# Moving the gates' running sums from VectorE to ScalarE and GpSimd, rebuilding the activation quarters from split halves, and four column chunks instead of five

## The chip, the cores and the metric

The kernel runs on one core of one Trainium2 chip. Its time is the device time of one execution in microseconds, from the first to the last instruction and what the device adds around it. Three runs of the kernel before took 1839.42, 1838.30 and 1839.01 us (median 1839.01 us).

The engines are called PE (TensorE, matrix products), DVE (VectorE), ACT (ScalarE), POOL (GpSimd) and SP (SyncE, which only issues transfers here). Each engine works through its own instructions in a fixed order, and a wait of one instruction holds all that stand behind it on that engine.

## The reference, cut to what matters

Two groups of tokens (128 context tokens and 512 latent tokens, 640 in all, width 1024) go through two layers with the same weights. Each layer:

```
mod = silu(cond) @ ada_w + ada_b                 # six vectors of 1024 per token group
sh_m, sc_m, g_m, sh_f, sc_f, g_f = six slices of mod
h = rmsnorm(x, norm_mix) * (1 + sc_m) + sh_m
y = token_mixers(h)                              # 4 gated-recurrence heads, 4 retention heads, w_out
x = x + g_m * y                                  # gate of the mixer
h = rmsnorm(x, norm_ffn) * (1 + sc_f) + sh_f
gate, up = split(h @ w_up)                       # 2 x 2816 columns
x = x + g_f * ((silu(gate) * up) @ w_down)       # gate of the feed-forward part
```

The vectors `g_m` and `g_f` are needed as rows of 1024 that lie on all 128 partitions, since `x` has tokens on the partitions. There are two of each per layer, one for each token group.

## The kernel before, in words

All products are done in pieces of full precision: an operand is split into a rounded part ("hi") and the rest ("lo"), and hi·hi, hi·lo and lo·hi are added up in PSUM. For the weights, `Stream.cut` does the split: the cast to `wh` on ACT (L103) and the subtraction to `wl` on DVE (L104). There are six raw weight buffers in the second layer and four split ones, and PE's use of a split buffer frees it.

A scheduler gives every engine its order ahead of time. What decides it here is the order in which the program emits the work (a main loop, with side lanes that advance one step each few microseconds of main work) and the scheduler's own estimate of when things are ready; buffer pools add waits.

**The gates** (`ada_gate`, `ada_chunk`) are a side lane. Each gate has two column halves of 512. For each half eight tiles `adw` (128 x 512 of `ada_w`, one for each k) are loaded through SP into the pool `adp`. DVE multiplies a tile by the condition's column k and adds it to `acc`, once for each token group: L510 for k = 0, L512 (one multiply-add) for the other seven. Then `hl`, the split of `acc` (L567, L568), goes through a product with a matrix of ones (`pg`, L571 and L572), which sums over the partitions and writes the sum on all of them; L574 adds it to the row `gate`. That is 128 DVE instructions for the two gates of both layers. The pool `adp` has two buffers; it also gives `sg` in `g_unit` and `xa` in `x_add`. The feed-forward gate (lane name `gf`) has to be finished in emission order before the first `w_down` pass of the layer, and the `pg` products of its second half stand in PE's order directly ahead of that pass.

**The feed-forward part.** In the first layer all 22 column blocks (128 columns of gate and of up each) are done plainly (`ws`). In the second layer only two are; the other 20 go through `seven`, which computes a pair of blocks from seven products instead of eight by sums of halves of the tokens and halves of the input width. `seven` needs four combinations `E` of four quarters `F` of the activations (a quarter is half of the tokens by half of the width, 128 x 1280 elements). `combos` (L654 to L657) forms them on DVE, `combo` splits each into hi (L665 on ACT) and lo (L666 on DVE). `combo_last` makes the one that PE's third product in a pair (`y0`, PSUM tile `sy`) reads, and writes it into a quarter of `hT`. PE's second product reads `E[2]`.

**The norm ahead of it.** After `w_out`, each of the five token tiles is normed, transposed on PE (`pt`, L598), scaled and shifted and split into `hT`. In the first layer `norm_c` does so through a temporary `full`. In the second `norm_f` writes the scaled values to the four quarters `hf` as well, so that they exist when `combos` starts; the tile t = 2 lies in both token halves and is done in two pieces of 64 columns.

**Chunks.** The 22 blocks are done in chunks (`CH`): after the blocks of a chunk, their rows of `w_down` are applied and the result is added to `x` (`x_add`, L1113 and L1115, 128 x 512 at a time; the last chunk does its second half in two times 256 columns). In the second layer there are five chunks of 5, 5, 4, 4 and 4 blocks, so the first holds the two plain blocks and three from `seven`.

Of the kernel before, what the change touches and what calls it, by code (L numbers as in the profile page):

```python
# [10 lines left out]
F32 = mybir.dt.float32  # L11
F32R = mybir.dt.float32r
I32 = mybir.dt.int32
AF = mybir.ActivationFunctionType
ALU = mybir.AluOpType
AX = mybir.AxisListType

P = 128
DM = 1024
KT = DM // P  # L20
NT = 5
TOK = NT * P
HALF = TOK // 2
# [4 lines left out]
NF = DFF // P  # L28
# [3 lines left out]
RAW_BUFS = 3  # L32
W_BUFS = 4
B_BUFS = 13
CH = ((11, 11), (5, 5, 4, 4, 4))
PLAIN = (NF, 2)
HK = KT // 2
LATE = "r2"
# [9 lines left out]
CUT = 256  # L48
Q_SCAN = 2.65
Q_ADA = (3.0, 2.0, 4.0)  # L50
ADP_BUFS = 2
BOOT_LOADS = (
    "L00 x4 L01 L10 L02 L11 L12 L13 L03 L20 x2 x3 x0 x1 L21 L30 L22 L31 L32 L33 L23 W W W "
).split()
# [93 lines left out]
class Net:  # L148
    def __init__(self, ctx, tc, a, o):
# [8 lines left out]
        self.wlp = pool("wlp", W_BUFS)  # L158
        self.adp = pool("adp", ADP_BUFS)
        self.smp = pool("smp", 4)  # L160
# [339 lines left out]
    def ada_chunk(self, l, col, alloc, sink):  # L500
        nc, a = self.nc, self.a
        acc = alloc("acc")
        for k in range(KT):
            w = self.adp.tile([P, 512], F32, tag="ad", name="adw")
            nc.sync.dma_start(out=w, in_=a["ada_w"][l, k * P:(k + 1) * P, col:col + 512])
            for c in range(2):
                d = acc[:, 512 * c:512 * c + 512]
                s = self.sT[:, c, k:k + 1]
                if k == 0:
                    self.pin(nc.vector.tensor_scalar(d, w, s, None, op0=ALU.mult))  # L510
                else:
                    nc.vector.scalar_tensor_tensor(d, w, s, d, op0=ALU.mult, op1=ALU.add)  # L512
            yield
        yield from sink(acc)

# [84 lines left out]

    def norm_c(self, t, src, l, m):
        nc = self.nc
        if m == 1 and PLAIN[l] < NF:
            return self.norm_f(t, src, l, m)
        km = KT // 2
        c = 0 if t == 0 else 1
        full = self.ON("full")
        fv = full[:, :DM].rearrange("p (k n) -> p k n", k=KT)
        sv = src[:, :DM].rearrange("p (k n) -> p k n", k=KT)
        G, S = self.modc[:, l, m, 0, c], self.modc[:, l, m, 1, c]  # L610
        hi, lo = self.hT[:, 0, :, t * P:(t + 1) * P], self.hT[:, 1, :, t * P:(t + 1) * P]
        for k in range(km):
            nc.scalar.activation(fv[:, k], sv[:, k], AF.Identity, bias=S[:, k:k + 1], scale=G[:, k:k + 1])
        bc = lambda v: v[:, km:].unsqueeze(2).to_broadcast([P, KT - km, P])
        nc.vector.tensor_tensor(fv[:, km:], sv[:, km:], bc(G), op=ALU.mult)
        nc.vector.tensor_tensor(fv[:, km:], fv[:, km:], bc(S), op=ALU.add)
        for a, b in ((0, km), (km, KT)):
            nc.scalar.copy(hi[:, a:b], fv[:, a:b])
            nc.vector.tensor_tensor(lo[:, a:b], fv[:, a:b], hi[:, a:b].bitcast(F32), op=ALU.subtract)

    def norm_f(self, t, src, l, m):
        nc = self.nc
        c = 0 if t == 0 else 1
        sv = src[:, :DM].rearrange("p (k n) -> p k n", k=KT)
        G, S = self.modc[:, l, m, 0, c], self.modc[:, l, m, 1, c]
        a = 0
        while a < P:
            h = (t * P + a) // HALF
            b = min(P, (h + 1) * HALF - t * P)
            n, o = b - a, t * P + a - h * HALF  # L630
            for kh in range(2):
                if (h, kh) not in self.F:
                    self.F[h, kh] = self.B("hf")
                fv = self.F[h, kh].rearrange("p (k n) -> p k n", k=HK)[:, :, o:o + n]
                ks = slice(HK * kh, HK * kh + HK)
                if kh == 0:
                    for k in range(HK):
                        nc.scalar.activation(fv[:, k], sv[:, k, a:b], AF.Identity, bias=S[:, k:k + 1],
                                             scale=G[:, k:k + 1])
                else:  # L640
                    bc = lambda v: v[:, ks].unsqueeze(2).to_broadcast([P, HK, n])
                    nc.vector.tensor_tensor(fv, sv[:, ks, a:b], bc(G), op=ALU.mult)
                    nc.vector.tensor_tensor(fv, fv, bc(S), op=ALU.add)
                hi, lo = (self.hT[:, d, ks, t * P + a:t * P + b] for d in range(2))
                nc.scalar.copy(hi, fv)
                nc.vector.tensor_tensor(lo, fv, hi.bitcast(F32), op=ALU.subtract)
            a = b

    def quarter(self, h, kh):
        return [self.hT[:, d, HK * kh:HK * kh + HK, h * HALF:(h + 1) * HALF] for d in range(2)]  # L650

    def combos(self):
        V, F = self.nc.vector, self.F
        V.tensor_tensor(F[1, 0], F[1, 1], F[1, 0], op=ALU.subtract)  # L654
        V.tensor_tensor(F[0, 0], F[0, 0], F[1, 0], op=ALU.add)
        V.tensor_tensor(F[1, 1], F[0, 0], F[1, 1], op=ALU.subtract)
        V.tensor_tensor(F[0, 1], F[0, 0], F[0, 1], op=ALU.subtract)  # L657
        self.E = {}
        for n, q in ((2, (0, 0)), (1, (1, 0)), (4, (0, 1))):
            self.E[n] = [self.B("eh", F32R).rearrange("p (k t) -> p k t", k=HK) for _ in range(2)]  # L660
            self.combo(q, *self.E[n])
# [537 lines left out]
    def ffn(self, l, mid):  # L1199
# [6 lines left out]
        f0 = 0  # L1206
        for ci, nch in enumerate(CH[l]):
            last = ci == len(CH[l]) - 1
            act = []
# [81 lines left out]
    def slots(self):  # L1291
# [23 lines left out]
        for l in range(DEPTH):  # L1315
# [12 lines left out]
            f0 = 0  # L1328
            for nch in CH[l]:
                for f in range(f0, f0 + nch):  # L1330
# [86 lines left out]
```

## Time and profile before

| | before |
|---|---|
| median of three runs | 1839.01 us |
| the profiled execution | 1836.8 us |
| its span, first to last instruction | 1835.0 us |
| PE busy | 1767.5 us, 96% of the span |
| DVE, ACT, POOL busy | 1215.7, 764.0 and 50.6 us |
| granted PE clock, mean of the span | 0.992 |

The span is 1.8 us shorter than the execution's own time. A busy PE is a pipeline with work in it; what can be shortened shows as idle time of PE, as the time in which its clock is granted at half speed, and as the start and the end of the kernel.

### The profile page before, as it was taken

What the parts mean: (1) busy time and instruction counts of PE and PEld (TensorE: products, weight loads), DVE (VectorE), ACT (ScalarE), POOL (GpSimd) and SP (SyncE); (2) the same over time, 40 slices, a digit from 0 to 9 for tenths busy, and PEclk for the clock granted to TensorE, in tenths of its full rate; (3) what the DMA queues carried; (4) which work ended last, traced back from release to release, by engine and by line L of the source; (5) the groups of instructions that cost most, each with busy time, mean ns of one, the idle gap of its engine ahead of it and who ended that gap; (6) DMA issues with size and microseconds to landing.
All of it is one profiled execution on the core that took longest, in us unless ns stands there. A gap on an engine that the chain in (4) does not pass through costs nothing.

```text
span 1835.0 us, 29181 instructions
## 1 busy us (share of the span) xinstructions
PE 1767.5 (96%) x11956; PEld 1676.0 (91%) x11956; DVE 1215.7 (66%) x1905; ACT 764.0 (42%) x1302; POOL 50.6 (3%) x59
## 2 busy tenths in 40 slices
PE   7999999999999999999999999999997799999997
PEld 5999999999999989999999999999896699889896
DVE  6787959755754555554466574776487676777776
ACT  7685545533422112222265464564353133233242
POOL 1100000000000000000000000000000000000000
PEclk9999999999999999999999999999999899999999
DMA  9424232222533444444222112322232223132231
GB/s 341 149 64 132 89 105 94 85 86 59 157 109 110 137 142 129 138 132 132 81 81 64 50 55 69 122 76 76 58 104 92 69 66 101 52 104 69 75 98 58
DMA packets 204358, 184.06 MB, mean 100 GB/s; under 512 B 7376, under 2 KB 171184, under 8 KB 204224
## 3 DMA queue, kind: packets, MB, share of 16 engines
q1 hardware_dynamic: 199328, 179.67, 31.1%
q10 hardware_dynamic: 4640, 2.43, 0.4%
q8 instruction: 94, 1.54, 0.3%
q14 instruction: 40, 0.33, 0.1%
q0 software_dynamic: 256, 0.09, 0.0%
HBM read 177.44 MB, written 4.72 MB: 99 GB/s over the span
## 4 chain that ended last, share of the span: by engine, by line
PE 78%; DVE 12%; ACT 5%; issue 3%; DMA 1%; POOL 1%; SPq 0%; DVEq 0%; POOLq 0%; ACTq 0%
PE gw L751 24%; PE ga L1170 6%; PE ga L1172 6%; PE ga L1171 6%; PE ga L797 4%; PE ga L796 4%; PE ga L795 4%; PE pl L888 3%; PE sx L684 2%; PE sx L685 2%; PE sx L686 2%; DVE wl L104 2%; PE sy L684 2%; PE sy L685 2%; PE sy L686 1%
## 5 line engine op out<-in xcount | busy, mean ns | idle before, releaser
L103 ACT CAST wh<-raw 128x1024 fp32r<-128x1024 f32 (+1 forms) x264 | 264.9, 1004 | 630.6 <-PE ga L1172 212.1
L104 DVE TENSOR_TENSOR wl<-raw,wh 128x1024 fp32r<-128x1024 f32 (+1 forms) x264 | 306.4, 1166 | 258.0 <-ACT wh L103 256.2
L751 PE MATMUL gw<-hT,wh 128*128 128x320 f32 x2432 | 461.9, 311 | 0.0
L751 PEld LDWEIGHTS gw<-hT,wh 128*128 128x128 f32 x2432 | 380.5, 188 | 0.6
L751 PE MATMUL gw<-hT,wl 128*128 128x320 f32 x1216 | 277.2, 309 | 0.0
L751 PEld LDWEIGHTS gw<-hT,wl 128*128 128x128 f32 x1216 | 203.1, 188 | 0.0
L795 PE MATMUL ga<-wh,hT 128*128 128x256 f32 x640 | 185.2, 289 | 0.0
L797 PE MATMUL ga<-wh,hT 128*128 128x256 f32 x640 | 181.3, 283 | 0.0
L796 PE MATMUL ga<-wl,hT 128*128 128x256 f32 x640 | 181.3, 283 | 0.0
L1170 PE MATMUL ga<-wh,act 128*128 128x512 f32 x365 | 145.2, 398 | 0.1
L1171 PE MATMUL ga<-wl,act 128*128 128x512 f32 x365 | 143.1, 392 | 0.0
L1172 PE MATMUL ga<-wh,act 128*128 128x512 f32 x365 | 141.3, 392 | 0.0
L795 PEld LDWEIGHTS ga<-wh,hT 128*128 128x128 f32 x640 | 122.5, 191 | 0.3
L796 PEld LDWEIGHTS ga<-wl,hT 128*128 128x128 f32 x640 | 122.5, 191 | 0.3
L797 PEld LDWEIGHTS ga<-wh,hT 128*128 128x128 f32 x640 | 122.3, 191 | 0.0
L546 DVE CUSTOM_DVE_ANT_0 junk<-adt,srow 128x1024 f32<-128x1024 f32 x96 | 117.1, 1220 | 1.5 <-ACT srow L531 0.2
L1113 DVE TENSOR_TENSOR xa<-ga,gate 128x512 f32<-128x512 f32 (+1 forms) x110 | 62.8, 589 | 41.6 <-PE ga L1172 17.8
L512 DVE SCALAR_TENSOR_TENSOR acc<-adw,sTt,acc 128x512 f32<-128x512 f32 x112 | 79.6, 746 | 15.2 <-DMA adw<-in_ada_w 15.2
L1170 PEld LDWEIGHTS ga<-wh,act 128*128 128x128 f32 x365 | 69.1, 189 | 18.7 <-DVE xa L1113 4.9
L1172 PEld LDWEIGHTS ga<-wh,act 128*128 128x128 f32 x365 | 69.1, 189 | 14.8
L1171 PEld LDWEIGHTS ga<-wl,act 128*128 128x128 f32 x365 | 69.1, 189 | 13.2
L684 PE MATMUL sx<-hT,wh 128*128 128x320 f32 x240 | 76.5, 322 | 3.3 <-DVE sv L694 3.0
(276 smaller groups left out, 3517.8 us busy)
## 6 DMA issues: line engine op xcount, KB each, us to landing
raw<-in_w_in SPq DMA_DIRECT2D x72, 512.0 KB, 3.8
adt<-in_ada_t SPq DMA_DIRECT2D x48, 512.0 KB, 3.8
raw<-in_w_up SPq DMA_DIRECT2D x48, 512.0 KB, 3.7
raw<-in_w_up SPq DMA_DIRECT2D x80, 256.0 KB, 3.0
raw<-in_w_down SPq DMA_DIRECT2D x39, 512.0 KB, 3.6
adw<-in_ada_w SPq DMA_DIRECT2D x64, 256.0 KB, 2.7
adw<-in_ada_w SPq DMA_DIRECT2D x16, 512.0 KB, 10.5
raw<-in_w_out SPq DMA_DIRECT2D x16, 512.0 KB, 3.7
```

The lines of the kernel that those rows point to most:

```text
L103: nc.scalar.copy(hi[:, :n], raw[:, :n])
L104: nc.vector.tensor_tensor(lo[:, :n], raw[:, :n], hi[:, :n].bitcast(F32), op=ALU.subtract)
L512: nc.vector.scalar_tensor_tensor(d, w, s, d, op0=ALU.mult, op1=ALU.add)
L546: r = V.tensor_tensor_reduce(out=self.junk, in0=w[:, :DM], in1=self.srow[c], scale=1.0, scalar=0.0, op0=ALU.mult, op1=ALU.add, accum_out=s ...
L684: mm(o, hi[:, k], h[0][:, k], start=first and k == 0, stop=False, skip_group_check=True)
L751: mm(o, w[:, k], self.hT[:, d, k, sl], start=k == 0 and i == 0, stop=k == KT - 1 and i == 2)
L795: mm(o, a_hi, hi[:, j], start=i == 0, stop=False)
L796: mm(o, a_hi, lo[:, j], start=False, stop=False)
L797: mm(o, a_lo, hi[:, j], start=False, stop=i == nk - 1)
L1170: mm(o, a_hi, hi[:, j], start=i == 0, stop=False)
L1171: mm(o, a_hi, lo[:, j], start=False, stop=False)
L1172: mm(o, a_lo, hi[:, j], start=False, stop=i == nk - 1)
```

## The change: what it does

Three things. The gates' multiply-adds leave DVE: ACT multiplies (`activation` with Copy and a scale per partition) and POOL adds, in all four gates; the products are tiles `prod` of the pool `adp`, which gets a third buffer. `norm_f` goes: the second layer's norm uses `norm_c` too, and `combos` first rebuilds the four quarters on DVE as hi + lo from `hT`, with four additions of 128 x 1280. The second layer's chunks become 6, 6, 5 and 5 blocks.

```diff
-CH = ((11, 11), (5, 5, 4, 4, 4))
+CH = ((11, 11), (6, 6, 5, 5))
...
-ADP_BUFS = 2
+ADP_BUFS = 3
...
             for c in range(2):
-                d = acc[:, 512 * c:512 * c + 512]
-                s = self.sT[:, c, k:k + 1]
-                if k == 0:
-                    self.pin(nc.vector.tensor_scalar(d, w, s, None, op0=ALU.mult))
-                else:
-                    nc.vector.scalar_tensor_tensor(d, w, s, d, op0=ALU.mult, op1=ALU.add)
+                d = av = acc[:, 512 * c:512 * c + 512]
+                if k:
+                    d = self.adp.tile([P, 512], F32, tag="ad", name="prod")
+                r = nc.scalar.activation(d, w, AF.Copy, scale=self.sT[:, c, k:k + 1])
+                if c == 0:
+                    self.pin(r)
+                if k:
+                    nc.gpsimd.tensor_tensor(av, av, d, op=ALU.add)
             yield
...
     def norm_c(self, t, src, l, m):
         nc = self.nc
-        if m == 1 and PLAIN[l] < NF:
-            return self.norm_f(t, src, l, m)
...
-    def norm_f(self, t, src, l, m):
...
     def combos(self):
         V, F = self.nc.vector, self.F
+        for q in ((1, 1), (1, 0), (0, 0), (0, 1)):
+            F[q] = self.B("hf")
+            hi, lo = self.quarter(*q)
+            V.tensor_tensor(F[q].rearrange("p (k t) -> p k t", k=HK), hi.bitcast(F32), lo.bitcast(F32), op=ALU.add)
         V.tensor_tensor(F[1, 0], F[1, 1], F[1, 0], op=ALU.subtract)
```

How the change moves instructions, at three places. Line numbers of the kernel before and after differ by up to 24; the names of the tiles are the same.

DVE, second layer, from the first plain blocks to the last combination (`hf` are the quarters, `eh` the lo parts of `E`, `sgf` and `act` the plain blocks' activations, `acc` the gate's running sum). Before:

```order
L512 SCALAR_TENSOR_TENSOR acc<-adw,sTt,acc 128x512 x4
L104 TENSOR_TENSOR wl<-raw,wh 128x1024
L656 TENSOR_TENSOR hf<-hf 128x1280
L657 TENSOR_TENSOR hf<-hf 128x1280
L666 TENSOR_TENSOR eh<-hf,eh 128x1280 x2
L512 SCALAR_TENSOR_TENSOR acc<-adw,sTt,acc 128x512
L666 TENSOR_TENSOR eh<-hf,eh 128x1280
L512 SCALAR_TENSOR_TENSOR acc<-adw,sTt,acc 128x512
L104 TENSOR_TENSOR wl<-raw,wh 128x512
L1224 TENSOR_TENSOR sgf<-sgf,gw 128x640
L666 TENSOR_TENSOR hT<-hf,hT 128x4x320
```

After:

```order
L1203 TENSOR_TENSOR act<-sgf,act 128x640
L629 TENSOR_TENSOR hf<-hT 128x1280
L104 TENSOR_TENSOR wl<-raw,wh 128x1024
L629 TENSOR_TENSOR hf<-hT 128x1280 x3
L630 TENSOR_TENSOR hf<-hf 128x1280
L104 TENSOR_TENSOR wl<-raw,wh 128x512
L631 TENSOR_TENSOR hf<-hf 128x1280
L1200 TENSOR_TENSOR sgf<-sgf,gw 128x640
L632 TENSOR_TENSOR hf<-hf 128x1280
L633 TENSOR_TENSOR hf<-hf 128x1280
L642 TENSOR_TENSOR eh<-hf,eh 128x1280 x3
L642 TENSOR_TENSOR hT<-hf,hT 128x4x320
```

Before, L654 and L655 (the first two combinations) stand further up, among the norm's last instructions; after, the four sums L629 and all of L630 to L633 stand behind the plain blocks' `act`, and three of the four sums behind the `wl` of a later weight tile.

The end of the first chunk of the second layer: the last part of the second half of `gf`. Before, on DVE (`sv` and `sgf` belong to the chunk's last pair of `seven`, its third):

```order
L104 TENSOR_TENSOR wl<-raw,wh 128x1024
L104 TENSOR_TENSOR wl<-raw,wh 128x512
L709 TENSOR_TENSOR sv<-sv,sy 128x320
L512 SCALAR_TENSOR_TENSOR acc<-adw,sTt,acc 128x512
L712 TENSOR_TENSOR sgf<-sgf,sv 128x640
L512 SCALAR_TENSOR_TENSOR acc<-adw,sTt,acc 128x512 x2
L714 TENSOR_TENSOR act<-sgf,act 128x640
L512 SCALAR_TENSOR_TENSOR acc<-adw,sTt,acc 128x512 x5
L568 TENSOR_TENSOR hl<-acc,hl 128x512
```

After, on ACT, around the last pair of the chunk, now its fourth:

```order
L510 ACTIVATE prod<-adw,sTt 128x512 x2
L103 CAST wh<-raw 128x1024
L678 ACTIVATE sgf<-sx 128x320
L510 ACTIVATE prod<-adw,sTt 128x512 x2
L103 CAST wh<-raw 128x1024
L681 ACTIVATE sgf<-sgf 128x320
L103 CAST wh<-raw 128x1024
L689 CAST act<-sgf 128x640
L510 ACTIVATE prod<-adw,sTt 128x512 x6
L569 CAST hl<-acc 128x512 x2
```

The accumulation was spread over DVE's last-pair work with five instructions left behind `act`; now the products of three whole tiles `adw` (k = 5, 6, 7) stand behind `act` on ACT.

POOL, the two mixers and what follows (`hs` is the heads' normalisation, `rs` the tokens'):

```order
-L955 TENSOR_TENSOR hs<-hs,hp 128x5 x8
-L592 TENSOR_TENSOR rs<-ms,hp 128x1 x10
-L955 TENSOR_TENSOR hs<-hs,hp 128x5 x8
-L592 TENSOR_TENSOR rs<-ms,hp 128x1 x10
-L1413 UNCONDITIONAL_BRANCH
-L1413 ISA
+L931 TENSOR_TENSOR hs<-hs,hp 128x5 x5
+L514 TENSOR_TENSOR acc<-acc,prod 128x512 x8
+L931 TENSOR_TENSOR hs<-hs,hp 128x5
+L514 TENSOR_TENSOR acc<-acc,prod 128x512 x14
+L931 TENSOR_TENSOR hs<-hs,hp 128x5
+L514 TENSOR_TENSOR acc<-acc,prod 128x512 x6
```

POOL had only the normalisations; now the 28 additions of a mixer gate stand ahead of the last three `hs` of the layer.

## Rows read from the trace of the kernel before

**Rows 1.** Page, part 1: busy us, share of the span, count.
```profile
PE 1767.5 (96%) x11956; PEld 1676.0 (91%) x11956; DVE 1215.7 (66%) x1905; ACT 764.0 (42%) x1302; POOL 50.6 (3%) x59
```

**Rows 2.** Stretches: stretch, length, busy PE PEld DVE ACT POOL, clock, DMA.
```profile
280.00:360.00 80.00, 76.23 (x602) 75.11 (x601) 67.50 (x105) 42.78 (x80) 3.62 (x2) 1.00 0.31 98
1160.00:1260.00 100.00, 97.32 (x773) 95.98 (x772) 83.95 (x133) 54.16 (x100) 3.07 (x2) 1.00 0.31 99
1340.00:1460.00 120.00, 94.17 (x555) 86.35 (x555) 92.45 (x137) 43.42 (x75) 1.96 (x3) 0.91 0.30 95
...
1440.00:1460.00 20.00, 14.81 (x49) 11.38 (x50) 9.69 (x14) 2.29 (x3) 0.00 (x0) 0.69 0.06 20
1500.00:1520.00 20.00, 19.66 (x130) 18.82 (x129) 16.74 (x26) 8.57 (x12) 0.00 (x0) 1.00 0.27 78
```

**Rows 3.** PE in order of time: start, us, line, tiles, idle before and releaser.
```profile
1354.67 1.06 PE L598 MATMUL pt<-ident,xn 128*128 128x128 f32 x8 [2.46 <-DVE xn L1192]
...
1385.38 0.41 PE L685 MATMUL sy<-hT,wh 128*128 128x320 f32 x1 [2.74 <-DVE hT L666]
1388.44 0.41 PE L684 MATMUL sx<-hT,wh 128*128 128x320 f32 x1 [1.19 <-DVE sv L694]
...
1400.77 0.59 PE L571 MATMUL pg<-hl,onesr 128*128 128x512 f32 x1 [2.60 <-ACT hl L567]
...
1418.17 0.80 PE L571 MATMUL pg<-hl,onesr 128*128 128x512 f32 x1 [3.58 <-ACT hl L567]
...
1444.48 0.79 PE L571 MATMUL pg<-hl,onesr 128*128 128x512 f32 x1 [10.73 <-ACT hl L567]
```

**Rows 4.** DVE in order of time, combinations of the second layer.
```profile
1359.29 1.49 DVE L654 TENSOR_TENSOR hf<-hf 128x1280 f32<-128x1280 f32 x1
...
1367.28 0.81 DVE L1224 TENSOR_TENSOR sgf<-sgf,gw 128x640 f32<-128x640 f32 x1
1368.10 1.22 DVE L104 TENSOR_TENSOR wl<-raw,wh 128x1024 fp32r<-128x1024 f32 x1
...
1376.97 2.89 DVE L666 TENSOR_TENSOR eh<-hf,eh 128x1280 fp32r<-128x1280 f32 x2
...
1383.84 1.48 DVE L666 TENSOR_TENSOR hT<-hf,hT 128x1280 fp32r<-128x1280 f32 x1
```

**Rows 5.** ACT in order of time, same stretch and the chunk's end.
```profile
1371.17 1.05 ACT L103 CAST wh<-raw 128x1024 fp32r<-128x1024 f32 x1 [2.32 <-PE gw L741]
...
1437.64 0.72 ACT L713 CAST act<-sgf 128x640 fp32r<-128x640 f32 x1 [3.01 <-DVE sgf L712]
```

**Rows 6.** Chain that ended last, at the end of the first chunk: start, us, what.
```profile
1440.36 2.58 DMA adw<-in_ada_w
```

**Rows 7.** Groups by line: busy us, mean ns of one, idle before.
```profile
L512 DVE SCALAR_TENSOR_TENSOR acc<-adw,sTt,acc 128x512 f32<-128x512 f32 x112 | 79.6, 746 | 15.2 <-DMA adw<-in_ada_w 15.2
...
L579 ACT ACTIVATE xa<-x 128x512 f32<-128x512 f32 x20 | 12.6, 630 | 28.8 <-DVE x L1115 28.8
...
L240 POOL MEMSET sr<- 128x1024 f32 x1 | 1.0, 951 | 0.0
```

**Rows 8.** POOL in order of time, two of the sixteen `hs`.
```profile
170.38 1.17 POOL L955 TENSOR_TENSOR hs<-hs,hp 128x5 f32<-128x5 f32 x1 [50.65 <-DVE hs L954]
...
351.37 2.01 POOL L955 TENSOR_TENSOR hs<-hs,hp 128x5 f32<-128x5 f32 x1 [52.47 <-DVE hs L954]
```

**Rows 9.** DVE in order of time, beside the second of these.
```profile
351.13 1.22 DVE L985 TENSOR_TENSOR QR<-QR,SW 128x1024 f32<-128x1024 f32 x1
```

**Rows 10.** DVE in order of time, the kernel's end.
```profile
1815.54 0.42 DVE L1113 TENSOR_TENSOR xa<-ga,gate 128x256 f32<-128x256 f32 x1 [0.56 <-PE ga L797]
...
1816.98 0.42 DVE L1113 TENSOR_TENSOR xa<-ga,gate 128x256 f32<-128x256 f32 x1 [0.56 <-PE ga L797]
...
1819.89 1.29 DVE L1283 SCALAR_TENSOR_TENSOR y<-x,rs,nf 128x1024 f32<-128x1024 f32 x1 [0.44 <-POOL rs L592]
...
1822.47 1.28 DVE L1283 SCALAR_TENSOR_TENSOR y<-x,rs,nf 128x1024 f32<-128x1024 f32 x1 [0.44 <-POOL rs L592]
```

More of the change, by code (lines that the diff above doesn't have):

```diff
@@ L619, in norm_c @@
             nc.vector.tensor_tensor(lo[:, a:b], fv[:, a:b], hi[:, a:b].bitcast(F32), op=ALU.subtract)
-    def norm_f(self, t, src, l, m):
[L622 to L647, printed above, removed]
     def quarter(self, h, kh):
```

## The prediction

> **What bounds the kernel now.** I read the page first, then stretches of 20 us, then the engines in order of time where PE has gaps. PE is busy in 96% of the span [rows 1], so moving work between the other engines pays only where PE waits, runs at its lower clock, or at the end. The stretches show one such place: 1340 to 1460 us, from the second layer's norm to the end of its first chunk. PE is busy for 94.17 of 120 us there, and at a mean clock of 0.91 [rows 2]. Two stretches in the mixers, where the mixer gates run, have 3.77 and 2.68 us of idle PE with VectorE busy for 84% [rows 2]. In the chunks that follow, a 20 us stretch has 0.34 us idle [rows 2].
>
> PE in order of time tells what the 26 us are [rows 3]: 2.46 for the last token tile's norm, 2.74 for the combination that `y0` reads, 1.19 for a `sv` on VectorE, and 2.60, 3.58 and 10.73 for the split sums of the gate `gf`. The page's sum over engines doesn't tell this: VectorE is busy for 66%, but bounds here because its order puts work ahead of what PE waits for.
>
> **The norm.** `norm_c` handles t = 2 in one piece. That shortens the run-up to the last tile's norm on VectorE and ScalarE. It can save nothing or all of the 2.46 us [rows 3]; I take the middle, 1.2.
>
> **The quarters.** What goes is the `hf` output of the norm, which cost no instruction of its own; what comes is four additions of 1280 elements. Two such instructions take 2.89 us [rows 4], so one occupies VectorE for 1.41. In the same stretch 14 accumulations of 0.746 us [rows 7] leave VectorE (first half of `gf`), 10.4 us against 5.6 added: by work alone this part gains. But the order decides. Before, the first combination starts at 1359.29 [rows 4], before the plain blocks are through. Now three of the four sums stand behind a `wl` whose cast needs the weight buffer that PE frees with the third plain block. That cast began at 1371.17, released by PE [rows 5]; with the earlier norm this is 1370.0. From there VectorE's order after the change, without a gap: cast 1.05 [rows 5], `wl` 1.14 (1.22 with 0.08 overlap), three sums 4.2, first combination 1.4, a half `wl` 0.6, second 1.4, `sgf` 0.7 [rows 4], third and fourth 2.8, three `eh` 4.2, the `hT` part 1.4 and 0.1 until PE sees it: 19.0 us, so 1389.0. Before, PE was ready for `y0` at 1382.64 and got it at 1385.38 [rows 3]. Now it starts 3.6 us later than before. That contains the gain of the norm. The wait is split: the second product needs `eh` of `E[2]` at about 1385, some 5 us after PE could take it, then 2 to 3 us for `y0`. I choose 3.6; with the norm's two ends it is 2.4 to 4.8.
>
> An idle PE of that length costs clock too. After the wait of 10.73 us the stretch 1440 to 1460 shows a clock of 0.69 [rows 2], between the levels of 1.2 and 2.4 GHz, and with 14.81 busy that is 4.6 us lost. After 5 us I bound it by 0 and 4.6 and take 1.0, since one of the slowed products ends inside the second wait. Back comes the 1.19 us for `sv` [rows 3]: PE is late then, and the accumulations ahead of `sv` are gone.
>
> **The gate's end.** The chunk now has a fourth `seven` pair, which gives the second half of `gf` more time, and VectorE no longer does it. The order on ScalarE takes both back: the products of k = 5, 6 and 7 stand behind the last pair's `act`. In three buffers one tile `adw` and two `prod` fit, so a tile's load waits for the products of the tile before it. Before, PE ended its last product at 1433.75 (1444.48 less 10.73 [rows 3]) and `act` on ScalarE ended at 1438.36 [rows 5], 4.6 us later. Without the accumulations between, less the wider weight tile that is now split there, I take 4.0. Then a product costs what an activation of 512 does, 0.63 [rows 7] (0.6 in a row). Behind `act`: two products 1.2, load 2.6 [rows 6], two products 1.2, load 2.6, one product 0.6, one addition, one cast 0.6, semaphores 0.3.
>
> The addition on GpSimd isn't in the trace. A memset of 1024 columns takes 0.95 us [rows 7], 0.48 for 512, which only writes; reading both inputs and writing, each at that rate and one after the other, would take 1.43. I take 0.95, two such passes. The sum is 4.0 + 9.1 + 0.95 = 14.0, against 10.73: 3.3 us more. Bounds: -1 (the last load already issued, `act` sooner) to +6 (GpSimd held up). The waits of 2.60 and 3.58 [rows 3] stay: they are for the buffer of `hl`, freed by the pair's own tail.
>
> The Trainium skill ("GPSIMD Engine Reference", Performance versus the Vector engine) states about 2.6 cycles of 1.2 GHz for an element of a two-input operation, so by an estimate 1.11 us for 512, and the sum below would be 0.2 us more. No row here shows it.
>
> **Chunks and the end.** One pass of `w_down` fewer saves one gap of 0.34 us [rows 2] and ten pairs of `x_add`, which lie beside PE. At the end, the last tiles' chain on VectorE advances every 2.58 us, while PE gives a tile every 1.44 us [rows 10] from 4 blocks, 1.8 from 5. PE's total is the same, so the chain starts 4 x 0.36 = 1.4 us earlier before PE's end. ScalarE has no wait there that grows.
>
> **The mixers.** Here 28 accumulations per gate leave VectorE, 20.9 us [rows 7] of 84 in 100 [rows 2], ScalarE gets 32 x 0.6 = 19 on top of 54, and GpSimd 28 additions ahead of three `hs` per layer, for which `on` and then PE's transposes wait. Gain at most the idle time, 6.45 us; loss: an `hs` behind an addition whose tile is still loading waits 2.6 + 0.6 + 0.95 = 4.2, and two of the six such `hs` reaching PE make 8. The queue on SP is touched too: raw weights stand behind `adw` loads that now wait for products, but six (in the first layer three) tiles are loaded ahead. I take 0.
>
> **The shared reads.** `hs` on GpSimd takes 1.17 us alone and 2.01 where VectorE has just begun an operation with two SBUF inputs; that operation keeps its 1.22 us [rows 8, 9]. So GpSimd was held and VectorE wasn't. The trace has no long GpSimd read, so what one does to VectorE is open: 0 to 0.95 us for each of the eight additions before `y0`'s combination. I take 1.0 in all.
>
> The Trainium skill ("SBUF — State Buffer", Who interferes with whom) says the two engines share ports under an exclusive lock: whichever comes first holds them, and the other is blocked for the whole instruction. The trace agrees for one direction, with 2.01 against 1.17. By it the other direction holds too, and the result is the first rival.
>
> **Sum.** Quarters and norm +3.6, clock +1.0, `sv` -1.2, gate's end +3.3, chunk -0.3, end -1.4, shared reads +1.0, mixers 0: +6.0. The profiled execution took 1836.8 us, so 1842.8; the median of the runs lies 2.2 above it, so 1845.0.
>
> **The rivals.** First, additions that hold VectorE. 112 of 0.95 us come, most where VectorE is dense. Seven more us before `y0` (eight additions, 1.0 already counted), and in the mixers VectorE would be at 84 - 21 + 27 = 90 of 100 instead of 84; I price the waits that this adds by doubling the idle time there, +6. That gives 1858. For it: the held `hs`; against it: VectorE's unchanged 1.22.
>
> Second, VectorE's work decides and not its order: the sums fill time in which it waited for PE's blocks. Before `y0` it has 10.4 - 5.6 = 4.8 us less to do, which removes the 2.74 at most; with the norm -3.9 instead of +3.6, no clock loss and no shared reads, the sum is -3.9 - 1.2 + 3.3 - 0.3 - 1.4 = -3.5: 1835.5. For it: 92.45 of 120 us busy [rows 2]; against it: the three sums behind the `wl`. It decides if `y0` starts less than 2.7 us after PE is ready.
>
> Third, and not slower either: the relief in the mixers. If their 6.45 us of idle go, the sum is -0.5: 1838.5. The point is whether the three `hs` per layer pass GpSimd without a wait over 2 us; for it VectorE's 84%, against it ScalarE going from 54 to 73.
>
> **How the numbers follow.** Two medians of this kernel can be told apart from about 0.2%, 3.7 us: 1835.3 to 1842.7 is no change. The forecast has 0.47, its own range 1840 to 1850; the first rival 0.18, the second 0.15, the third 0.12, and 0.08 for larger losses in the mixers. Faster: half of the second, a third of the third and little else, 0.14. Within: the rest of these two and a tenth of the forecast, 0.22. Slower: 0.64. The range from 1833 to 1860 leaves out part of the second and the worst mixers.
>
> **What would show it.** `E[2]` and `y0`: idle PE of 7 to 9 us in place of 2.74. Last `pg`: about 14 in place of 10.73, with two loads of `adw` in the chain between products. `prod` 0.6 us, additions near 0.95; longer ones beside VectorE's two-input operations, and VectorE's lengthened or not, decide the first rival. The mixers' two stretches: idle 4 to 9 us together. The forecast is wrong if `y0` waits under 3 us, if the products of k = 5 to 7 run before `act`'s end, or if the mixers move by over 6 us.

## The result and the profile after

The changed kernel takes 1886.28 us (median of 4 runs, 1885.47 to 1888.62) against 1838.65: 1.0262 times as long, with a 95% interval of 1.0245 to 1.0280. The loss of 47.6 us was forecast as 6. Its profiled execution took 1888.6 us with a span of 1886.8.

Part 1 of the page after: busy us, share, count, as in [rows 1].

```profile
PE 1785.2 (95%) x11971; PEld 1691.4 (90%) x11971; DVE 1166.5 (62%) x1758; ACT 843.5 (45%) x1425; POOL 210.5 (11%) x171
```

VectorE has 49 us less to do, and the kernel is slower. PE is busy 17.7 us longer with 15 matmuls more, so its lower clock (0.980 in the mean, 0.992 before) costs about that; the other 34 us of the 51.8 us longer span are idle PE. So about a third of the loss is clock, for which my sum had 1.0.

Where the time goes, by the starts of GpSimd's `hs` and `rs` operations, one of each stage: the mixer of the first layer (fifth `hs` to the last `rs` of its norm), the first FFN, the second layer's mixer (to the fourth `rs` of its norm), the last tile's norm (to the fifth), the second FFN (to the kernel's last `rs`). POOL in order of time, after: start, us, line, idle before and releaser.

```profile
270.13 1.17 POOL L931 TENSOR_TENSOR hs<-hs,hp 128x5 f32<-128x5 f32 x1 [25.16 <-DVE hs L930]
...
1380.43 1.46 POOL L594 TENSOR_TENSOR rs<-ms,hp 128x1 f32<-128x1 f32 x1 [4.93 <-DVE ms L592]
```

The same rows of every trace give this table (us of a stage; the kernel before in the first line):

| kernel | mixer 1 | FFN 1 | mixer 2 | norm | FFN 2 |
|---|---|---|---|---|---|
| before | 197.8 | 472.1 | 407.7 | 7.0 | 476.9 |
| after | 209.4 | 476.2 | 419.3 | 5.5 | 501.2 |
| gates only | 209.1 | 476.7 | 416.7 | 7.0 | 503.3 |
| quarters and chunks | 197.7 | 472.1 | 407.8 | 5.5 | 483.1 |
| additions on VectorE | 198.3 | 473.4 | 410.2 | 7.0 | 491.0 |
| additions that only write | 202.3 | 473.3 | 410.5 | 5.5 | 489.2 |
| chunks and third buffer | 197.8 | 472.0 | 407.2 | 7.0 | 470.6 |

The norm's 1.5 us came close to the 1.2 of the forecast. The mixers lose 11.6 us each, where I had 0; the second FFN loses 24.3. The stretches after, columns as in [rows 2]; the first is the same stretch as the first there:

```profile
280.00:360.00 80.00, 70.63 (x520) 69.59 (x519) 53.16 (x72) 55.51 (x94) 30.80 (x22) 0.94 0.28 90
...
1400.00:1420.00 20.00, 10.49 (x63) 9.53 (x62) 18.16 (x13) 9.96 (x12) 7.67 (x4) 0.84 0.12 37
1420.00:1440.00 20.00, 16.72 (x79) 15.19 (x78) 14.11 (x16) 8.02 (x13) 11.82 (x6) 0.73 0.33 102
...
1500.00:1520.00 20.00, 6.92 (x15) 4.79 (x16) 3.58 (x5) 4.70 (x8) 7.46 (x6) 0.51 0.12 38
```

From 1400 to 1420 us VectorE is busy for 18.16 us with only 13 instructions. Most of these are long in any case; which ones are lengthened, its rows in order of time tell, with GpSimd's in the fence behind them:

```profile
1402.41 2.20 DVE L104 TENSOR_TENSOR wl<-raw,wh 128x1024 fp32r<-128x1024 f32 x1 [1.84 <-ACT wh L103]
1404.53 5.38 DVE L629 TENSOR_TENSOR hf<-hT 128x1280 f32<-128x1280 f32 x3
1409.84 2.54 DVE L630 TENSOR_TENSOR hf<-hf 128x1280 f32<-128x1280 f32 x1
...
1417.84 4.28 DVE L642 TENSOR_TENSOR eh<-hf,eh 128x1280 fp32r<-128x1280 f32 x3
```

```profile
1400.97 2.55 POOL L514 TENSOR_TENSOR acc<-acc,prod 128x512 f32<-128x512 f32 x2 [3.88 <-ACT prod L510]
1405.91 5.12 POOL L514 TENSOR_TENSOR acc<-acc,prod 128x512 f32<-128x512 f32 x2 [2.39 <-ACT prod L510]
1420.90 6.79 POOL L514 TENSOR_TENSOR acc<-acc,prod 128x512 f32<-128x512 f32 x2 [9.87 <-ACT prod L510]
```

A `wl` of 1024 takes 1.22 us [rows 4]; the one at 1402.41 begins inside a pair of additions and takes 2.20: it ends 1.09 us, about its own time, after the pair does at 1403.52. The three sums at 1404.53 take 5.38, where the three operations of the same size at 1417.84 take 4.28. The combination at 1409.84 takes 2.54 where 1.48 is normal. The other way round, a pair of additions takes 2.55 us by itself and 5.12 and 6.79 beside VectorE's row of combinations. Each engine holds the other. PE's waits in order of time (columns as in [rows 3]):

```profile
1415.73 0.63 PE L660 MATMUL sx<-eh,wh 128*128 128x320 f32 x1 [7.13 <-ACT eh L641]
1417.86 0.63 PE L660 MATMUL sy<-hT,wh 128*128 128x320 f32 x1 [1.50 <-ACT hT L641]
...
1423.58 0.64 PE L661 MATMUL sy<-hT,wh 128*128 128x320 f32 x1 [0.91 <-DVE hT L642]
...
1511.98 0.79 PE L573 MATMUL pg<-hl,onesr 128*128 128x512 f32 x1 [17.99 <-ACT hl L569]
```

These answer to 2.74 and 10.73 in [rows 3]. At the combinations PE waits for 10.4 us in all (with 0.88 in the part left out). Not all of that is holding: in the run below in which GpSimd mostly writes, PE waits there for 7.2. In the second mixer the same thing is seen at one wait of 4.08 us of PE for `QS`. VectorE and then GpSimd, after:

```profile
1203.51 1.91 DVE L932 TENSOR_TENSOR on<-O,hs 128x640 f32<-128x640 f32 x1 [1.29 <-POOL hs L931]
1205.34 2.28 DVE L104 TENSOR_TENSOR wl<-raw,wh 128x1024 fp32r<-128x1024 f32 x1
1207.54 0.81 DVE L823 TENSOR_TENSOR QS<-QS,gw 128x640 f32<-128x640 f32 x1
```

```profile
1202.30 1.18 POOL L931 TENSOR_TENSOR hs<-hs,hp 128x5 f32<-128x5 f32 x1 [2.78 <-DVE hs L930]
1203.45 3.09 POOL L514 TENSOR_TENSOR acc<-acc,prod 128x512 f32<-128x512 f32 x2
```

The additions come just before `on`, which is ready 0.06 us later; `on` and `wl`, in front of `QS` in VectorE's order, are each held for about the length of an addition (1.91 in place of 0.82, and 2.28 in place of 1.22). `hs` had not stood behind an addition here: it was VectorE that was late.

In the first mixer PE's longest wait is another, 4.71 us for `X`, which ScalarE copies. The chain that ended last there, start, us, what:

```profile
302.50 2.16 POOL acc L514
...
304.67 3.42 DMA adw<-in_ada_w
...
309.05 1.30 POOL acc L514
...
310.37 2.59 DMA adw<-in_ada_w
...
314.38 0.90 ACT X L850
...
316.23 1.86 PE pl L864 x7
```

The copy stands in ScalarE's order behind the products of two tiles. Each tile's load begins when an addition of the tile before has ended, and the first of these additions took 2.16 us in place of 1.27. So ScalarE waited for loads, and PE for ScalarE.

At the second FFN gate's end the chain that ended last runs through one tile after another in the same way: start, us, what.

```profile
1499.47 0.73 ACT prod L510
...
1500.33 1.27 POOL acc L514
1501.62 2.62 DMA adw<-in_ada_w
...
1504.32 0.73 ACT prod L510
...
1505.18 1.27 POOL acc L514
1506.47 2.59 DMA adw<-in_ada_w
```

The load begins 0.02 us after the addition ends, not after the products: 4.85 us a tile, where my working had 1.2 and 2.6.

### The profile page after: what moved, and what is told of

It reads as the page before. It is cut to its first block, busy times and chain, and to the rows that moved or that the text cites. A ratio compares the mean times of both kernels' runs of the same rounds, so it can differ in the third digit from the quotient of the medians.

```text
span 1886.8 us, 29334 instructions
## 1 busy us (share of the span) xinstructions
PE 1785.2 (95%) x11971; PEld 1691.4 (90%) x11971; DVE 1166.5 (62%) x1758; ACT 843.5 (45%) x1425; POOL 210.5 (11%) x171
## 4 chain that ended last, share of the span: by engine, by line
PE 70%; DVE 11%; ACT 8%; DMA 4%; issue 3%; POOL 3%; POOLq 0%; SPq 0%; DVEq 0%; ACTq 0%
PE gw L727 19%; PE ga L1146 5%; PE ga L1147 5%; PE ga L1148 5%; DMA adw<-in_ada_w 4%; PE ga L773 3%; PE ga L772 3%; PE ga L771 3%; PE sx L660 3%; PE pl L864 2%; POOL acc L514 2%; PE sx L661 2%; PE sx L662 2%; DVE wl L104 2%; PE sy L660 2%
## 5 line engine op out<-in xcount | busy, mean ns | idle before, releaser
L104 DVE TENSOR_TENSOR wl<-raw,wh 128x1024 fp32r<-128x1024 f32 (+1 forms) x265 | 322.6, 1221 | 307.1 <-ACT wh L103 305.5
L514 POOL TENSOR_TENSOR acc<-acc,prod 128x512 f32<-128x512 f32 x112 | 161.4, 1461 | 283.9 <-ACT prod L510 283.9
L1146 PE MATMUL ga<-wh,act 128*128 128x512 f32 x360 | 142.5, 396 | 0.0
L1148 PE MATMUL ga<-wh,act 128*128 128x512 f32 x360 | 139.5, 392 | 0.0
L594 POOL TENSOR_TENSOR rs<-ms,hp 128x1 f32<-128x1 f32 x25 | 15.7, 628 | 938.3 <-DVE ms L592 938.3
L510 ACT ACTIVATE prod<-adw,sTt 128x512 f32<-128x512 f32 x112 | 75.1, 716 | 65.4 <-DMA adw<-in_ada_w 64.8
L864 PE MATMUL pl<-X 128*128 128x128 f32 x560 | 74.0, 280 | 10.1 <-ACT X L851 10.0
```

Of the source, the lines that this page charges most:

```text
L104: nc.vector.tensor_tensor(lo[:, :n], raw[:, :n], hi[:, :n].bitcast(F32), op=ALU.subtract)
L514: nc.gpsimd.tensor_tensor(av, av, d, op=ALU.add)
L864: nc.tensor.matmul(pl[:, i * P:(i + 1) * P], X[:, TOK + i * P:TOK + (i + 1) * P], X[:, i * P:(i + 1) * P], start=True, stop=True)
L1146: mm(o, a_hi, hi[:, j], start=i == 0, stop=False)
L1148: mm(o, a_lo, hi[:, j], start=False, stop=i == nk - 1)
```

## The experiments

Theory A: GpSimd's additions and VectorE's operations with two SBUF inputs stop each other. Rival B: the longer chain of a tile (load, product, addition, load) in three buffers is the cost, whoever adds. Rival C: the rebuilt quarters carry the second FFN's loss. Each result is a ratio to the kernel before on the same chip, with its 95% interval.

**Gates only.** Before, with the gates' sums as changed and `ADP_BUFS = 3`; norm, combinations and chunks as before.

> The kernel before with the gates' sums alone moved (products on ScalarE, additions on GpSimd, three buffers); quarters and chunks as before. Theory A (GpSimd's additions and VectorE's operations with two SBUF inputs hold each other up): the mixers' loss, about 11.6 us in each, and the gate's end come from here, so 1865 to 1880 us, with VectorE operations of twice their length beside additions. Rival C (the rebuilt quarters carry the second layer's FFN loss of 24 us): the mixers' 23 and the first FFN's 4 only, so 1864 to 1867, with no loss in the second FFN beyond the gate's end (7 us). Either way a value under 1850 would say that the parts only hurt together.

1891.32 us, 1.0282 (1.0268 to 1.0296). More than either theory wanted, and no less than the whole change: rival C falls. The second FFN (503.3) loses as much without the quarters as with them.

**Quarters and chunks.** The changed kernel with the old inner loop and `ADP_BUFS = 2`.

> The changed kernel with the gates' sums back on VectorE in two buffers: quarters rebuilt from the halves and four chunks remain. Theory A: nothing beside the combos is held up, so 1837 to 1845 (norm 1.5 shorter, the start of y0 up to 4 later, chunks within 1 of zero). Rival C: 1850 to 1862, since the second FFN keeps most of its 24 us.

1840.9 us, 1.0010 (1.0001 to 1.0019), as A had it. PE in order of time at the combinations:

```profile
1386.95 0.64 PE L658 MATMUL sx<-eh,wh 128*128 128x320 f32 x1 [5.54 <-ACT eh L639]
1389.09 0.64 PE L658 MATMUL sy<-hT,wh 128*128 128x320 f32 x1 [1.50 <-ACT hT L639]
1390.60 0.64 PE L659 MATMUL sx<-eh,wh 128*128 128x320 f32 x1 [0.88 <-DVE eh L640]
1395.54 0.64 PE L659 MATMUL sy<-hT,wh 128*128 128x320 f32 x1 [1.64 <-DVE hT L640]
```

The sum is 9.6 us in place of 2.74. The forecast for this step, 7 to 9, is missed by 0.6 us with GpSimd out of it and the sums back on VectorE.

**Chunks only.** `CH = ((11, 11), (6, 6, 5, 5))` in the kernel before.

> The kernel before with four chunks (6, 6, 5, 5) in the plain pairs instead of five. Theory A and rival C alike: within 1 us of the kernel before, 1837.5 to 1839.5; my sum had -0.3 for it. A theory that the chunks hurt would give 1842 or more.

1835.76 us, 0.9979 (0.9969 to 0.9989): faster by 3.9 by the ratio, outside what I expected. PE's four longest waits for `pg` in the second FFN are 12.6 us together in place of 17.6, the longest 5.2 in place of 10.73. That fits a fourth pair which gives the gate's sums time; no run tests this by itself.

**Additions on VectorE.**

```diff
-                    nc.gpsimd.tensor_tensor(av, av, d, op=ALU.add)
+                    nc.vector.tensor_tensor(av, av, d, op=ALU.add)
```

> As the first run, but the additions on VectorE instead of GpSimd (the products stay on ScalarE, the same three buffers, the same order of loads). Theory A: without GpSimd at the shared port most of the loss goes: 1840 to 1850, no lengthened VectorE operations; what is left is ScalarE's queue waiting for loads and the longer chain of a tile. Rival B (the chain load, product, addition, load in three buffers is the cost, whoever adds): 1860 or more, the mixers' landmarks late as in the changed kernel.

1855.93 us, 1.0091 (1.0077 to 1.0105): between the two. The mixers are back to within 2.5 us, so their loss came with the additions on GpSimd. But 14 us stay in the second FFN, which A alone doesn't explain. ScalarE in order of time at the gate's end shows them:

```profile
1447.76 1.33 ACT L510 ACTIVATE prod<-adw,sTt 128x512 f32<-128x512 f32 x2 [2.76 <-DMA adw<-in_ada_w]
1451.98 1.33 ACT L510 ACTIVATE prod<-adw,sTt 128x512 f32<-128x512 f32 x2 [2.88 <-DMA adw<-in_ada_w]
1456.04 1.33 ACT L510 ACTIVATE prod<-adw,sTt 128x512 f32<-128x512 f32 x2 [2.73 <-DMA adw<-in_ada_w]
```

With one weight tile and two products in three buffers, load and products follow one another, 4.1 us a tile. So B holds too, for a part.

**Additions that only write, and additions of 4 columns.** The first has both edits below, the second the first line only.

```diff
-                    nc.gpsimd.tensor_tensor(av, av, d, op=ALU.add)
+                    nc.gpsimd.tensor_tensor(av[:, :4], av[:, :4], d[:, :4], op=ALU.add)
+                    for _ in range(2):
+                        nc.gpsimd.memset(av, 0.0)
```

> The changed kernel, but each addition on GpSimd is replaced by one over 4 columns and two memsets of 512, so GpSimd is held about as long (some 1.2 us by the 0.95 that a memset of 1024 took) but reads next to nothing; the gates' sums are left out. Theory A (VectorE's operations with two SBUF inputs and GpSimd's reads hold each other up): VectorE's lengthened operations vanish, the mixers lose at most 3 us each as with the additions on VectorE (0.6 and 2.5), and what stays is the gate's end: 1853 to 1868. Rival B (the length of the chain load, product, addition, load): the additions last as long as before, so the mixers keep about 11 us each and the time stays at 1878 or more.

> The changed kernel, but each addition covers 4 of 512 columns, so GpSimd is held for a small part of the time and all dependences stay; the gates' sums are left out. Theory A: close to the run with memsets, less three times about 1 us at the gate's end: 1848 to 1864. Rival B: here too 1848 to 1864, because the chain is short now; so the two runs side by side decide: B wants them 15 us or more apart, A within 6.

1859.09 us, 1.0105 (1.0086 to 1.0125), and 1854.36 us, 1.0082 (1.0059 to 1.0104): 4 us apart, where B wanted 15. GpSimd's groups with memsets (busy us, mean ns of one), then VectorE's `wl` in that run and in the changed kernel (duration ns min/median/max):

```profile
L516 POOL MEMSET acc<- 128x512 f32 x224 | 114.4, 525 | 7.0
L514 POOL TENSOR_TENSOR acc<-acc,prod 128x4 f32<-128x4 f32 x112 | 33.0, 294 | 266.8 <-ACT prod L510 266.8
```

```profile
L104 DVE TENSOR_TENSOR wl<-raw,wh x265: 418/1224/1229, 38.0 to 1832.3; 128x1024 fp32r<-128x1024 f32 x125, 128x512 fp32r<-128x512 f32 x5, 128x256 fp32r<-128x256 f32 x2, 128x768 fp32r<-128x768 f32 x1
```

```profile
L104 DVE TENSOR_TENSOR wl<-raw,wh x265: 417/1224/2318, 36.9 to 1860.6; 128x1024 fp32r<-128x1024 f32 x125, 128x512 fp32r<-128x512 f32 x5, 128x256 fp32r<-128x256 f32 x2, 128x768 fp32r<-128x768 f32 x1
```

GpSimd is busy for 147 us in the same places as it was for 161 with additions, and no `wl` takes more than 1.229 us (2.318 before that). VectorE's 1758 instructions keep it busy for 1132.3 us in all, 34.2 less than the same instructions in the changed kernel. The reads are all but gone, and 29 of the 47.6 us with them. That speaks for A, but the run also shortens B's chain: the short addition frees the buffer ahead of the memsets, so a tile at the gate's end takes 3.9 us in place of 4.85. How much of the 29 us is due to that, the next run bounds. The expected 3 us at most in a mixer was missed by the first one, 4.6.

**Second product in place.**

```diff
-                if k:
+                if k and c:
+                    d = w
+                elif k:
                     d = self.adp.tile([P, 512], F32, tag="ad", name="prod")
```

> The changed kernel, but the product of the second column half is written over its weight tile, so a tile takes two of the three buffers and the next load is issued a tile earlier. Theory A: the mixers keep their 11 us each, since the additions still read beside VectorE; only the gate's end loses some of its loads (up to 2 x 2.6 us): 1876 to 1886. Rival B: the load is out of the chain, so 1850 to 1868.

1878.57 us, 1.0206 (1.0182 to 1.0230), as A had it: the mixers keep 11.6 and 15.1 us, the second FFN gains 7. ScalarE's products (busy, mean ns, idle before and what ended it), in the changed kernel and then in place, where the line counts the first products alone:

```profile
L510 ACT ACTIVATE prod<-adw,sTt 128x512 f32<-128x512 f32 x112 | 75.1, 716 | 65.4 <-DMA adw<-in_ada_w 64.8 <-ACT Sr L921 0.5
L512 ACT ACTIVATE prod<-adw,sTt 128x512 f32<-128x512 f32 x56 | 40.3, 719 | 19.0 <-DMA adw<-in_ada_w 10.2 <-POOL acc L516 8.1 <-ACT S L923 0.5
```

Most of the wait for loads is gone, and only about 10 of the 48 us (1.0262 to 1.0206) with it. So waiting for loads behind additions is the small part of the loss, and the memsets' 29 us are for the most part the reads: the two runs together decide for A.

**In place, and additions on VectorE.** Both edits above in the kernel before, with four chunks.

> Products on ScalarE, the second written over its weight tile, additions on VectorE, three buffers, four chunks, quarters as before. In the run with additions on VectorE the last six tiles of the gate followed each other every 4.1 us: a load of 2.8 us and two products of 1.33 together, one after the other. If that row of loads is what is left without GpSimd's reads, it overlaps now and the gate's end loses about 6 x 1.3 us; with the chunks' 3 us 1841 to 1848. If ScalarE's order is what is left (products behind the pair's other work), no more than the chunks' 3: 1851 to 1855.

1843.09 us, 1.0016 (1.0006 to 1.0025). ScalarE's group of first products (idle before and what ended it), with additions on VectorE and three buffers, then in place:

```profile
L510 ACT ACTIVATE prod<-adw,sTt 128x512 f32<-128x512 f32 x112 | 75.1, 716 | 47.9 <-DMA adw<-in_ada_w 47.7
```

```profile
L512 ACT ACTIVATE prod<-adw,sTt 128x512 f32<-128x512 f32 x56 | 40.3, 720 | 8.9 <-DMA adw<-in_ada_w 8.1 <-DVE acc L516 0.7
```

The wait for loads falls from 47.7 to 8.1 us, and the time by 14, of which the chunks make 4. That is the part of B. What is left is neither: with the same chunks and buffers, and product and addition in one VectorE instruction as before the change, the run with chunks and third buffer below takes 0.9949, 12.3 us less. Products on ScalarE with additions on VectorE cost that much; where, is open.

**Copies instead of additions.** `nc.gpsimd.tensor_copy(av, d)` in place of the addition: one SBUF operand read.

> The changed kernel, but each addition on GpSimd is replaced by a copy of the product, one SBUF operand read instead of two; the gates' sums are left out. If any read by GpSimd holds VectorE's operations with two inputs, the lengthened operations stay (2.2 us in place of 1.22) and the time is 1868 to 1886. If it takes two operands, it is as with memsets: 1853 to 1863.

1859.77 us, 1.0105 (1.0091 to 1.0118). By time it is the run with memsets, but not by its rows. VectorE, then GpSimd, in order of time:

```profile
1385.87 4.70 DVE L629 TENSOR_TENSOR hf<-hT 128x1280 f32<-128x1280 f32 x3
1390.49 1.89 DVE L630 TENSOR_TENSOR hf<-hf 128x1280 f32<-128x1280 f32 x1
```

```profile
1387.66 3.38 POOL L514 COPY acc<-prod 128x512 f32<-128x512 f32 x2 [3.22 <-ACT prod L510]
...
1400.88 5.47 POOL L514 COPY acc<-prod 128x512 f32<-128x512 f32 x2 [9.85 <-ACT prod L510]
```

Copies are held too (two of 0.61 us take 5.47), and VectorE's operations are lengthened by 0.4 us, not by 1.06. So neither expectation holds as written: a copy contends, but for less than half as long as an addition. VectorE is busy for 1135.5 us, 3.2 more than with memsets, and next to that run the time doesn't show it.

**Third buffer, chunks, and quarters again.** `ADP_BUFS = 3` in the kernel before; with four chunks; and with the quarters besides (the sums on VectorE in all).

> The kernel before with a third buffer for the gates' weight tiles and nothing else. If the third buffer and the chunks add up, 1831 to 1836, with a last wait for pg of 5 to 8 us in place of 10.73. If the chunks alone bring the gain (more pairs to hide the sums behind), 1837 to 1840.

> The kernel before with four chunks and a third buffer for the gates' weight tiles; the sums stay on VectorE. In the kernel before PE waited 2.60, 3.58 and 10.73 us for the split sums of the last gate, with a load of 2.58 us on the last chain. If loads set the gate's end, 1826 to 1833; if the order on VectorE does, as with four chunks alone, 1834 to 1838.

> The changed kernel with the gates' sums back on VectorE, the third buffer kept: it differs from the kernel before with chunks and third buffer (1830.0) by the rebuilt quarters alone. My sum had +3.4 for these (3.6 for the quarters and the norm, 1.0 for the clock, -1.2 for sv): 1832 to 1836. The rival that VectorE's work decides wants 1826 to 1830.

1834.15 us, 0.9969 (0.9957 to 0.9981); 1829.98 us, 0.9949 (0.9935 to 0.9964); 1836.56 us, 0.9984 (0.9975 to 0.9993). Buffer and chunks add up: 5.7 and 3.9 us, 9.4 together. With the buffer alone the last wait for `pg` is 8.4 us, just above the expected 5 to 8. The quarters cost 0.0035 of the time, 6.4 us, where my sum had 3.4, so the third run lies just above its 1832 to 1836; its waits at the combinations are 8.3 us together, within 7 to 9. All three beat both kernels, the second by most.

## Why the prediction was wrong

The direction was right, the size was not: +6.0 against +47.6. Split by the ratios (48.2 in all): 28.9 us are the difference between additions and memsets (1.0262 to 1.0105), 17.5 between memsets and the sums on VectorE in two buffers (to 1.0010), 1.8 the rest. The third buffer, worth 5.7 us by itself, had no term in my sum.

A second way through the runs gives nearly the same: chunks and third buffer -9.4, products on ScalarE in place +12.3, their additions moved on from VectorE to GpSimd +28.5, quarters +6.4, a buffer of its own for the second product +10.3. The 28.5 is an estimate: it takes the quarters' 6.4 us from runs with the sums on VectorE.

**The failed step: the shared reads, +1.0.** It measured 28.9, of which the buffer that the memset run frees earlier is a part, by the run in place at most about 10; the second way, without that part, has 28.5. I saw a held `hs` beside an unchanged VectorE operation [rows 8, 9] and took the other direction, which I had called open, at next to nothing. But there VectorE had come first; the trace of before has no long read by GpSimd that comes first. I counted only eight additions, those before `y0`, when 112 were to come.

**The mixers, 0.** They measured 23.2, far over the 6 us that I had named as a sign of being wrong; most of it is the step above again, since with memsets they lose 7.4. I looked for `hs` behind an addition. What was late was VectorE in front of `QS` and `on` in the second mixer, and in the first ScalarE's copy to `X`, behind products that waited for loads; then PE's clock: it was 0.94 from 280 to 360 us, where it had been 1.00 [rows 2]. I had given ScalarE 19 us more work there and asked only how busy it is, not what stands behind a product whose tile isn't there yet. The first FFN's gate, for which I had no term, lost 4.1.

**The first rival** had the mechanism and a chance of 0.18. Its 13 us were too small: it doubled 6.45 us of idle in two stretches, and took VectorE's loss alone. GpSimd is held as well, an addition of 1.27 us for up to 5.1, and the next load stands behind that addition.

**The gate's end, +3.3.** The wait is 17.99, not 14.0. The order was as forecast: behind `act`, two tiles with a load each and a third tile. But the first product behind `act` began 5.5 us after PE's end (1499.47 less 1493.99), not 4.0: two `wl` and `sgf` on VectorE lay ahead of `act`, and one of these `wl` was held beside additions, 2.15 in place of 1.22. And the next load takes a buffer that an addition, not a product, frees, so each of the two tiles takes 4.85 us, not 3.8. With memsets in place of the additions the wait is 14.20. The addition's 0.95 was low; it takes 1.27 undisturbed. The Trainium skill ("GPSIMD Engine Reference", Performance versus the Vector engine) gives by an estimate 1.11, nearer but low too. The clock of 0.51 from 1500 to 1520 us came on top, which my 1.0 for the clock did not hold.

**Quarters, norm, `sv`, clock at `y0`: +3.4** measured 6.4. The waits were about as forecast (9.6 and, with the third buffer, 8.3 us for 7 to 9), the norm gained 1.5; the clock after the wait was under-priced: from 1372 to 1412 us it was 0.77 and 0.76 in two stretches of 20 us, against 1.00 and 0.91 in the run without rebuilt quarters. **Chunks and end, -1.7**, measured -3.9.

The rule in the Trainium skill ("SBUF — State Buffer", Who interferes with whom), that the two engines share ports under an exclusive lock for a whole instruction, agrees with the trace in both directions: 1.22 becomes 2.20, and 2.55 becomes 6.79. It also says there that a GpSimd operation that only writes doesn't contend; the memsets agree, with 525 ns each and no `wl` over 1.229 us. I had cited the first and priced it as the less likely case.

## What to carry to other kernels

Moving elementwise work with SBUF inputs to GpSimd takes less off VectorE than it seems on paper, as long as VectorE runs operations with two SBUF inputs at the same time: count all the new operations, not only those in front of the one wait you look at, and price those that meet such an operation at up to their own length. Here 112 additions lengthened VectorE's work by 34 us. In an engine's fixed order, ask too what stands behind an instruction that waits for a load: here that was the copy to `X`. When a sum is split over two engines with a buffer between them, ask who frees the buffer of the next load; here the second product in place let the load overlap. Idle PE is paid twice where it lowers the clock, so look at the granted clock in the stretch of each new wait.

## What the runs showed of the hardware

Back-to-back operations of VectorE with two SBUF inputs can shut GpSimd out for several of them, even when its own is short. In the run with additions of 4 columns (0.20 us each), GpSimd, then VectorE:

```profile
1392.94 4.18 POOL L514 TENSOR_TENSOR acc<-acc,prod 128x4 f32<-128x4 f32 x2 [11.26 <-ACT prod L510]
```

```profile
1394.09 1.48 DVE L642 TENSOR_TENSOR hT<-hf,hT 128x1280 fp32r<-128x1280 f32 x1
1395.49 0.81 DVE L1203 TENSOR_TENSOR act<-sgf,act 128x640 fp32r<-128x640 f32 x1
1396.23 0.68 DVE L112 TENSOR_TENSOR raw<-raw 128x512 f32<-128x512 f32 x1
1396.83 0.48 DVE L670 TENSOR_TENSOR sv<-sx,sv 128x320 f32<-128x320 f32 x1
```

Two operations of 0.20 us end at 1397.12, shortly after the first VectorE operation with an input from PSUM (`sx`) begins at 1396.83. At other places an addition came between two operations of the row, as at 1405.91 after; which of the two it is was not settled.
